# A hybrid layer on one core: opening loads in rows of 4 KB, and zeros multiplied on TensorE before the first block

## The chip, the core and the metric

The kernel runs on one NeuronCore of a Trainium2 chip. The core has a matrix engine (TensorE, PE in the profile, with its weight loads as PEld), a vector engine (VectorE, DVE), an engine for functions and copies (ScalarE, ACT), a general engine (GpSimd, POOL) and a synchronising engine (SyncE, SP) that here issues most loads. Each engine works through its own list of instructions in order and waits on semaphores for the others. Loads and stores go through 16 DMA engines. Work happens in SBUF, 128 partitions wide; TensorE writes into the eight banks of PSUM, each 128 partitions by 512 fp32 numbers.

The metric is the device time of one execution in microseconds. The kernel before took 1743.69 us in the median of three runs (1743.11, 1743.69, 1744.18).

## The reference: what is computed

One decoder layer, batch 1, 2048 positions, model width 1024, all in fp32, cut to what matters:

```python
cond = silu(c)                                  # one vector of 1024
mod = cond @ w_ada + b_ada                      # 6 x 1024: shift, scale, gate, twice
sh1, sc1, g1, sh2, sc2, g2 = split(mod, 6)

h = x * (1 + sc1) + sh1
z = h @ w_in                                    # 1024 -> 2048
gate_b, gate_c, v_conv, v_pool = split(z, 4)
y_conv = gate_b * short_conv(gate_c * v_conv, conv_w)      # causal, width 3
y_pool = multiscale_pool(v_pool, w_pool, pool_scale)       # windows 2, 4, 8, 16
mix = concat(y_conv, y_pool) @ w_out
x = layer_norm(alpha * x + (1 + g1) * mix)

h = x * (1 + sc2) + sh2
f = square(relu(h @ w_mlp_in)) @ w_mlp_out      # 1024 -> 4096 -> 1024
x = layer_norm(alpha * x + (1 + g2) * f)
```

Nothing of the layer can start before the first scales and shifts: they need `silu(c)`, and the dot product of it with rows of `w_ada`.

## The kernel before, in words

The sequence is worked on in two blocks of 1024 positions. The feature dimension lies on the partitions, 8 tiles of 128. The big products (input projection, output projection, MLP) are made on TensorE from operands that are split into a high and a low part (`split`, `mm3`: three matmuls for one product), and several of them in a scheme with sums of blocks that needs seven products of blocks instead of eight. Loads, splits and sums run beside the matmuls. The order of instructions on each engine is fixed when the kernel is built: the scheduler of the framework puts the instructions in an order by what it expects to be ready, and the program holds it in some places with `issue_after`.

The change touches only the opening of the program.

- `vecs` holds all small vectors, `c` among them. It is the first load. `in_turn` chains the loads that follow it on SP's queue in the order of the code.
- The first column tile of `w_ada` for the scale and for the shift of the first 128 features (`first`, two tiles of 128x1024) is loaded in four halves, then the first 128 rows of the first group's input weights (`w0`, 128x512), then the first 128 features of `x` (`x0`, in two halves of 128x512).
- `silu(c)` is made on ScalarE and VectorE. `spread` broadcasts it over all partitions with eight transposes on TensorE against the identity matrix, four into each of two PSUM banks (`cond_banks`).
- Behind the transposes, `WARM` = 7 multiplications of the identity by itself fill TensorE; nobody reads what they write.
- `ada_first` multiplies the tiles of `first` with the banks in four products on VectorE, each with a running sum (the sums go to `part`), and two small additions make the first scale and shift (`mod[:, 0:2]`).
- `first_group` then goes over the 8 feature tiles k. For each it needs the scale and shift of that tile; ScalarE makes the high part of `x * scale + shift` in two halves (`shifted`), VectorE the low part, and TensorE does 24 matmuls of 128x128 by 128x512 into 8 banks. While it does, `loads(k + 1)` brings the next tile's two rows of `w_ada`, weights and `x`, and VectorE makes the next scale and shift (`dot`, `biased`).

Names in the rows: `h_` are tiles of 128x1024 (the two of `first`, and operands), `r_` raw weights, `o_` other 128x1024 tiles (`x0` is one), `w_` split weights, `ps_` PSUM banks, `tmp` a scratch tile of 128x512.

Of the kernel before, what the change touches and what calls it, by code (L numbers as in the profile page):

```python
# [8 lines left out]
F32 = mybir.dt.float32  # L9
F32R = mybir.dt.float32r  # L10
AF = mybir.ActivationFunctionType
ALU = mybir.AluOpType

P = 128
# [3 lines left out]
H = 512  # L18
# [9 lines left out]
WINDOWS = (2, 4, 8, 16)  # L28
HALO = 16
HALF_SUMS = (1, 2, 3, 3, 3, 3, 3, 0)  # L30
WARM = 7
WW = T + HALO

SC1, SH1 = 0, 1
# [4 lines left out]


@with_exitstack
def tile_hybrid_layer(ctx: ExitStack, tc: tile.TileContext, xT, x, wada, vec, win0, win,
                      wins, wpool, wout, wmix, w1, w2, rows, out):
    nc = tc.nc

# [10 lines left out]
    def mk(p, shape, dt, tag, bufs):  # L56
        names[0] += 1
        return p.tile(shape, dt, name=f"{tag}_{names[0]}", tag=tag, bufs=bufs)

    def t_h(dt=F32R):  # L60
        return mk(big, [P, T], dt, "h", 28)

    def t_o(w=T, dt=F32):
        return mk(big, [P, w], dt, "o", 10)

    def t_w(dt=F32R):
        return mk(big, [P, T], dt, "w", 6)

    def t_r():
        return mk(big, [P, T], F32, "r", 5)  # L70

    def t_ps():
        return mk(pp, [P, H], F32, "ps", 8)
# [14 lines left out]
    def tt(out_, a, b_, op):  # L88
        return nc.vector.tensor_tensor(out_, a, b_, op=op)  # L89


    vecs = cp.tile([P, 104], F32, name="vecs")
# [3 lines left out]
    def in_turn(dst, src):  # L96
        if before:
            with tc.issue_after(before.pop()):
                d = nc.sync.dma_start(dst, src)  # L99
        else:  # L100
            d = nc.sync.dma_start(dst, src)
        before.append(d.ins)

    in_turn(vecs[:, :88], vec)
    halves = [slice(h * H, h * H + H) for h in range(2)]
    x0 = t_o()
    first = [t_h(F32), t_h(F32)]
    w0 = t_r()
    for hs in halves:
        for i, f in enumerate((SC1, SH1)):  # L110
            in_turn(first[i][:, hs], wada[f][:, hs])
    in_turn(w0[:, :H], win0[0])
    for hs in halves:
        in_turn(x0[:, hs], xT[0, 0][:, hs])
    silu = cp.tile([P, KD], F32, name="silu")
    nc.scalar.activation(silu, vecs[:, VX : VX + KD], AF.Sigmoid)
    tt(silu, silu, vecs[:, VX : VX + KD], ALU.mult)
# [3 lines left out]
    mod = cp.tile([P, 48], F32, name="mod")  # L121
    ident = cp.tile([P, P], F32, name="ident")
# [16 lines left out]
            nc.scalar.copy(dst[:, hs], banks[h])  # L139

    cond_banks = spread(silu)

    warm = t_ps()
    for _ in range(WARM):
        nc.tensor.matmul(warm[:, :P], ident, ident, start=True, stop=True)
    small = cp.tile([P, 6], F32, name="small")
    part, epst, c15 = small[:, 0:4], small[:, 4:5], small[:, 5:6]
    nc.gpsimd.memset(c15, 1.5)
# [21 lines left out]
    cond = t_o(D)  # L170

    def ada_first():
        for i in range(2):
            for h, hs in enumerate(halves):
                nc.vector.scalar_tensor_tensor(
                    first[i][:, hs], first[i][:, hs], 1.0, cond_banks[h], op0=ALU.mult, op1=ALU.mult,
                    accum_out=part[:, 2 * h + i : 2 * h + i + 1])
        nc.vector.tensor_tensor(part[:, 0:2], part[:, 0:2], vecs[:, 0:2], op=ALU.add)
        return nc.vector.tensor_tensor(mod[:, 0:2], part[:, 0:2], part[:, 2:4], op=ALU.add)

    opened = []
# [5 lines left out]
    def biased(f0, f1):  # L187
        return nc.vector.tensor_tensor(mod[:, f0:f1], acc[:, f0:f1], vecs[:, f0:f1], op=ALU.add)
# [14 lines left out]


    def shifted(dst, r, k, cs):
        return nc.scalar.activation(dst[:, cs], r[:, cs], AF.Identity, bias=mod[:, 2 * k + SH1 : 2 * k + SH1 + 1],  # L206
                                    scale=mod[:, 2 * k + SC1 : 2 * k + SC1 + 1])

    def load_m(src):
# [124 lines left out]
    def first_group(A):  # L334
        ps = {}

        def loads(k):
            rows_ = [t_h(F32) for _ in range(2)]
            wr, a = t_r(), t_o()
            for i, r in enumerate(rows_):  # L340
                in_turn(r, wada[2 * k + i])
            in_turn(wr[:, :H], win0[k])
            in_turn(a, xT[0, k])
            return rows_, wr, a

        done = ada_first()
        wr, a = w0, x0
        for k in range(KD):
            wt = t_w()
            hi, lo = t_h(), t_h()  # L350
            A.append((hi, lo))
            opened.append(done.ins)
            if k == 0:
                nc.scalar.copy(wt[:, :H], wr[:, :H])
            with tc.issue_after(done.ins):
                if k:
                    nc.scalar.copy(wt[:, :H], wr[:, :H])
                tt(wt[:, H:], wr[:, :H], wt[:, :H].bitcast(F32), ALU.subtract)
                for hs in halves:
                    high = shifted(hi, a, k, hs)  # L360
                    if k:
                        shifted(a, a, k, hs)
            if k + 1 < KD:
                rows_, wr_n, a_n = loads(k + 1)
            if k == 0:
                with tc.issue_after(high.ins):
                    for hs, bank in zip(halves, cond_banks):
                        nc.scalar.copy(cond[:, hs], bank)
            elif k + 1 < KD:
                done = dot(2 * k + 2, rows_[0])  # L370
            with tc.issue_after(done.ins):
                for hs in halves:
                    if k == 0:
                        sc, sh = (mod[:, 2 * k + i : 2 * k + i + 1] for i in (SC1, SH1))
                        nc.vector.tensor_scalar(a[:, hs], a[:, hs], sc, sh, op0=ALU.mult, op1=ALU.add)
                    low = tt(lo[:, hs], a[:, hs], hi[:, hs].bitcast(F32), ALU.subtract)
            if k + 1 < KD:
                with tc.issue_after(low.ins):
                    for i in range(k > 0, 2):
                        dot(2 * k + 2 + i, rows_[i])  # L380
                done = biased(2 * k + 2, 2 * k + 4)
                wr, a = wr_n, a_n
            for h, hs in enumerate(halves):
                for p in range(3):
                    for m in range(4):
                        if k == 0 and p == 0:
                            ps[m, h] = t_ps()
                        w = (H if p == 1 else 0) + m * P
                        nc.tensor.matmul(ps[m, h], wt[:, w : w + P], A[k][p // 2][:, hs],  # L389
                                         start=k == 0 and p == 0, stop=k == KD - 1 and p == 2)  # L390
        return ps
# [873 lines left out]
def _lay(inputs):  # L1265
    import numpy as np

    a = {k: np.asarray(v) for k, v in inputs.items()}
    x = a["x"].reshape(S, D)
    sh1, sc1, g1, sh2, sc2, g2 = [a["w_ada"][0].T.reshape(6, KD, P, D)[i] for i in range(6)]  # L1270
    vsh1, vsc1, vg1, vsh2, vsc2, vg2 = [a["b_ada"][0].reshape(6, KD, P)[i] for i in range(6)]

    def pairs(p, q):
        return np.stack([p, q], axis=1).reshape((2 * KD,) + p.shape[1:])

    wada = np.concatenate([pairs(sc1, sh1), g1, pairs(sc2, sh2), g2])
    bada = np.concatenate([pairs(vsc1, vsh1), vg1, pairs(vsc2, vsh2), vg2])
    conv = a["conv_w"][0].reshape(3, NG, P).transpose(1, 0, 2).reshape(3 * NG, P)
    vec = np.concatenate([bada, conv, a["pool_scale"][0].reshape(NG, P),
                          a["ln1_g"][0].reshape(KD, P), a["ln1_b"][0].reshape(KD, P),  # L1280
                          a["c"].reshape(KD, P)]).T
    w = a["w_in"][0].reshape(KD, P, 4, NG, P)[:, :, [3, 1, 2, 0]]
    return {
        "xT": x.T.reshape(KD, P, NB, T).transpose(2, 0, 1, 3),
        "x": x,
        "wada": wada,
        "vec": vec,
        "win0": w[:, :, :, 0].reshape(KD, P, 4 * P),
        "win": w.transpose(3, 2, 1, 0, 4).reshape(NG, 4, P, KD * P),
        "wins": w.reshape(2, 4, P, 2, 2, NG, P).transpose(5, 4, 0, 2, 3, 1, 6).reshape(NG, 4, P, T),  # L1290
        "wpool": a["w_pool"][0].transpose(0, 2, 1),
        "wout": a["w_out"][0][: D // 2].reshape(2, 2, P, 2, H).transpose(3, 0, 2, 1, 4),
        "wmix": a["w_out"][0][D // 2 :].reshape(NG, P, D),
        "w1": a["w_mlp_in"][0].reshape(2, 4, P, NC, 2, 2, P).transpose(3, 5, 0, 2, 4, 1, 6).reshape(NC, 4, P, T),
        "w2": a["w_mlp_out"][0].reshape(NC, 2, 2, P, 2, H).transpose(0, 2, 4, 3, 1, 5).reshape(NC, 4, P, T),
        "rows": np.stack([a["ln1_g"][0], a["ln1_b"][0], a["ln2_g"][0], a["ln2_b"][0]]),
    }
# [18 lines left out]
```

## Time and profile before

| what | value |
|---|---|
| median of three runs | 1743.69 us (1743.11 to 1744.18) |
| span of the profiled execution, first to last instruction | 1741.3 us |
| what lies around the span, median less span | 2.4 us |
| mean granted clock of TensorE | 0.997 |
| TensorE busy | 1726.9 us, 99% of the span |
| VectorE busy | 1265.7 us, 73% |
| ScalarE busy | 857.3 us, 49% |
| GpSimd busy | 191.7 us, 11% |
| the chain that ended last: TensorE's share | 98% |
| first real matmul | 10.07 us after the start |

The profiled execution has no time of its own beside its span; the 2.4 us are the distance of the span to the median of the runs. The profile's times count from the first instruction. A row of the timeline gives the start, the length of the group, engine, line of the code, operation, written tile `<-` read tiles, shape, how many; in square brackets stands the idle time of the engine ahead of it and what ended it. A row of a cut into stretches gives the stretch, its length, the busy time and count of each engine in the order PE, PEld, DVE, ACT, POOL, then the clock that TensorE was granted (1.00 is full), the busy share of the DMA engines and their rate in GB/s. In the view of one line of code the three figures are the shortest, median and longest duration in ns, then the first and last start.

### The profile page before, as it was taken

The page shows a single profiled execution, that of the slowest core. Times are in us where ns is not written, and L with a number is a line of the kernel's source. Part 1 is how long each engine was busy: PE and PEld are TensorE (multiplying, and loading weights), DVE is VectorE, ACT ScalarE, POOL GpSimd, SP SyncE. Part 2 cuts the span into 40 slices and gives each one's busy share as a digit, 9 for nine tenths or more (in the row PEclk, how much of TensorE's full clock was granted, in tenths as well). Part 3 has the DMA queues.
Part 4 walks back from the last instruction along what each step waited for, and adds up shares of the span by engine and source line. Part 5 has one row for each costly group of instructions (what it writes and reads, how often), then busy time and mean ns, then how long its engine had stood idle before and what let it go on. Part 6 is the DMA issues. An engine that isn't in the chain of part 4 may idle for free.

```text
span 1741.3 us, 21294 instructions
## 1 busy us (share of the span) xinstructions
PE 1726.9 (99%) x7678; PEld 1430.4 (82%) x7678; DVE 1265.7 (73%) x1617; ACT 857.3 (49%) x1158; POOL 191.7 (11%) x373
## 2 busy tenths in 40 slices
PE   8999999999999999999999999999999999999997
PEld 7888888888888888888888888888888888888886
DVE  7898698877777686759686789695565656465885
ACT  5323358554445554446573345765455564344451
POOL 0212221122222000000000000101000100000000
PEclk9999999999999999999999999999999999999999
DMA  9888777768888999887572266655434479677771
GB/s 377 332 334 326 302 260 275 271 253 322 315 332 312 378 419 340 295 281 269 200 265 82 100 230 218 226 193 199 143 133 145 158 269 371 194 248 251 269 256 49
DMA packets 136907, 443.70 MB, mean 255 GB/s; under 512 B 15713, under 2 KB 16225, under 8 KB 136801
## 3 DMA queue, kind: packets, MB, share of 16 engines
q1 hardware_dynamic: 94752, 292.90, 47.3%
q0 software_dynamic: 42048, 149.44, 22.4%
q8 instruction: 60, 0.98, 0.2%
q14 instruction: 47, 0.38, 0.1%
HBM read 307.54 MB, written 134.74 MB: 254 GB/s over the span
## 4 chain that ended last, share of the span: by engine, by line
PE 98%; DVE 1%; DMA 0%; ACT 0%; SPq 0%; issue 0%; DVEq 0%; ACTq 0%
PE ps L86 31%; PE ps L84 31%; PE ps L85 31%; PE ps L389 3%; PE ps L740 1%; DVE o L89 0%; DMA r<-in_win 0%; DVE o L1197 0%; DVE o L1191 0%; DVE st L709 0%; PE ps L132 0%; SPq L99 0%; ACT mv L700 0%; DVE mv L713 0%; ACT h L206 0%
## 5 line engine op out<-in xcount | busy, mean ns | idle before, releaser
L85 PE MATMUL ps<-h,w 128*128 128x512 f32 x1312 | 510.3, 389 | 0.0
L86 PE MATMUL ps<-h,w 128*128 128x512 f32 x1312 | 510.3, 389 | 0.0
L84 PE MATMUL ps<-h,w 128*128 128x512 f32 x1312 | 510.0, 389 | 0.0
L84 PE MATMUL ps<-h,h 128*128 128x512 f32 x1120 | 436.1, 389 | 0.0
L86 PE MATMUL ps<-h,h 128*128 128x512 f32 x1120 | 435.9, 389 | 0.0
L85 PE MATMUL ps<-h,h 128*128 128x512 f32 x1120 | 435.7, 389 | 0.0
L79 ACT CAST h<-r 128x1024 fp32r<-128x1024 f32 (+1 forms) x184 | 186.8, 1019 | 312.0 <-PE ps L85 201.2
L80 DVE TENSOR_TENSOR h<-r,h 128x1024 fp32r<-128x1024 f32 (+1 forms) x184 | 216.1, 1179 | 109.4 <-ACT h L79 109.2
L85 PEld LDWEIGHTS ps<-h,w 128*128 128x128 f32 x1312 | 246.3, 188 | 51.6 <-DVE h L80 0.4
L79 ACT CAST w<-r 128x1024 fp32r<-128x1024 f32 x156 | 164.3, 1053 | 252.4 <-PE ps L85 243.8
L86 PEld LDWEIGHTS ps<-h,w 128*128 128x128 f32 x1312 | 246.3, 188 | 51.2 <-DVE w L80 0.3
L84 PEld LDWEIGHTS ps<-h,w 128*128 128x128 f32 x1312 | 246.1, 188 | 51.4 <-issue 0.2
L80 DVE TENSOR_TENSOR w<-r,w 128x1024 fp32r<-128x1024 f32 x156 | 190.4, 1222 | 109.7 <-ACT w L79 108.3
L86 PEld LDWEIGHTS ps<-h,h 128*128 128x128 f32 x1120 | 210.2, 188 | 43.7
L85 PEld LDWEIGHTS ps<-h,h 128*128 128x128 f32 x1120 | 210.3, 188 | 43.7
L84 PEld LDWEIGHTS ps<-h,h 128*128 128x128 f32 x1120 | 210.3, 188 | 43.4 <-DVE o L859 0.3
L89 DVE TENSOR_TENSOR o<-o,o 128x512 f32<-128x512 f32 (+1 forms) x170 | 162.1, 958 | 57.2 <-DMA usum<-o 47.0
L89 DVE TENSOR_TENSOR o<-o,ps 128x512 f32<-128x512 f32 x156 | 105.5, 682 | 57.1 <-PE ps L86 56.3
L80 DVE TENSOR_TENSOR h<-w,h 128x1024 fp32r<-128x1024 f32 x112 | 136.4, 1218 | 6.2 <-ACT h L79 6.2
L79 ACT CAST h<-w 128x1024 fp32r<-128x1024 f32 x112 | 117.6, 1050 | 8.5 <-DMA w<-in_w 7.4
L965 POOL DMA_DIRECT2D usum<-o x112 | 59.9, 535 | 522.9 <-ACT o L962 226.4
L89 DVE TENSOR_TENSOR r<-r,r 128x1024 f32<-128x1024 f32 x60 | 73.4, 1223 | 22.0 <-DMA r<-in_w 15.5
(138 smaller groups left out, 1184.4 us busy)
## 6 DMA issues: line engine op xcount, KB each, us to landing
usum<-o POOLq DMA_DIRECT2D x112, 512.0 KB, 4.9
r<-usum SPq DMA_DIRECT2D x112, 512.0 KB, 5.0
w<-w2sum SPq DMA_DIRECT2D x64, 512.0 KB, 6.4
r<-in_w SPq DMA_DIRECT2D x60, 512.0 KB, 5.0
w<-in_w SPq DMA_DIRECT2D x48, 512.0 KB, 6.5
o<-in_w SPq DMA_DIRECT2D x72, 256.0 KB, 6.0
w2sum<-o POOLq DMA_DIRECT2D x64, 256.0 KB, 6.7
h<-in_wada SPq DMA_DIRECT2D x22, 512.0 KB, 9.6
```

Of the source, the lines that this page charges most:

```text
L79: high = nc.scalar.copy(hi, src)
L80: return high.ins, nc.vector.tensor_tensor(lo, src, hi.bitcast(F32), op=ALU.subtract).ins
L84: nc.tensor.matmul(ps, whi, xhi, start=first, stop=False, skip_group_check=goes_on)
L85: nc.tensor.matmul(ps, whi, xlo, start=False, stop=False, skip_group_check=goes_on)
L86: nc.tensor.matmul(ps, wlo, xhi, start=False, stop=last, skip_group_check=goes_on)
L89: return nc.vector.tensor_tensor(out_, a, b_, op=op)
L389: nc.tensor.matmul(ps[m, h], wt[:, w : w + P], A[k][p // 2][:, hs], start=k == 0 and p == 0, stop=k == KD - 1 and p == 2)
L740: nc.tensor.transpose(ps[:, t * P : t * P + P], R[4 * h + t][:, k * P : k * P + P], ident)
L965: nc.gpsimd.dma_start(usum[g, i], r)
```

## The change

Two things are done to the opening.

First, the loads. A new input `opening` of 3 x 128 x 1024 is laid out on the host: the first slab holds the left halves (columns 0 to 511) of the scale tile and of the shift tile side by side, the second the right halves, the third the first weights beside the left half of `x0`. Each is loaded by one DMA with rows of 4 KB, where there were seven DMAs with rows of 2 KB; the right half of `x0` still comes in a DMA of its own. Since a slab now holds one half of both tiles, the products of `ada_first` go by slab, and the first small addition stands inside the loop. In `first_group` the first x comes as two separate pieces (one inside `w0`), so the code there takes a list of pieces.

Second, TensorE. A tile of zeros is filled by VectorE at the program's start, and `warming(EARLY)` multiplies it by itself 10 times ahead of the code for `silu`; `warming(WARM)` does so 14 times behind the transposes in the code, where the 7 multiplications of the identity stood.

```diff
-WARM = 7
+EARLY, WARM = 10, 14
...
-    x0 = t_o()
     first = [t_h(F32), t_h(F32)]
-    w0 = t_r()
-    for hs in halves:
-        for i, f in enumerate((SC1, SH1)):
-            in_turn(first[i][:, hs], wada[f][:, hs])
-    in_turn(w0[:, :H], win0[0])
-    for hs in halves:
-        in_turn(x0[:, hs], xT[0, 0][:, hs])
+    w0, x0 = t_r(), t_o()
+    for r, src in zip((first[0], first[1], w0), opening):
+        in_turn(r, src)
+    in_turn(x0[:, H:], xT[0, 0][:, H:])
+    zeros = t_tmp()[:, :P]
+    nc.vector.memset(zeros, 0.0)
+    warm = t_ps()
+
+    def warming(n):
+        for _ in range(n):
+            nc.tensor.matmul(warm[:, :P], zeros, zeros, start=True, stop=True)
+
+    warming(EARLY)
     silu = cp.tile([P, KD], F32, name="silu")
...
     cond_banks = spread(silu)
-
-    warm = t_ps()
-    for _ in range(WARM):
-        nc.tensor.matmul(warm[:, :P], ident, ident, start=True, stop=True)
+    warming(WARM)
...
     def ada_first():
-        for i in range(2):
-            for h, hs in enumerate(halves):
+        for h in range(2):
+            for i, hs in enumerate(halves):
                 nc.vector.scalar_tensor_tensor(
-                    first[i][:, hs], first[i][:, hs], 1.0, cond_banks[h], op0=ALU.mult, op1=ALU.mult,
+                    first[h][:, hs], first[h][:, hs], 1.0, cond_banks[h], op0=ALU.mult, op1=ALU.mult,
                     accum_out=part[:, 2 * h + i : 2 * h + i + 1])
-        nc.vector.tensor_tensor(part[:, 0:2], part[:, 0:2], vecs[:, 0:2], op=ALU.add)
+            if h == 0:
+                nc.vector.tensor_tensor(part[:, 0:2], part[:, 0:2], vecs[:, 0:2], op=ALU.add)
         return nc.vector.tensor_tensor(mod[:, 0:2], part[:, 0:2], part[:, 2:4], op=ALU.add)
...
-        wr, a = w0, x0
+        wr, a = w0, [w0[:, H:], x0[:, H:]]
...
+    sides = np.concatenate([sc1[0], sh1[0]], axis=1).reshape(P, 2, 2, H)
+    opening = np.stack([np.concatenate([sides[:, 0, h], sides[:, 1, h]], axis=1) for h in range(2)]
+                       + [np.concatenate([w[0, :, :, 0].reshape(P, 4 * P), x.T[:P, :H]], axis=1)])
```

The order in which TensorE gets its instructions doesn't follow the code here, since the scheduler sets it. TensorE's first rows before, from the start of the program (L132 is a transpose, with the identity and `silu` as operands; L145 is the multiplication of the identity; L389 the layer's first matmuls; in brackets what an instruction waits for):

```order
L132 MATMUL ps_94<-ident,silu 128x128 [waits DVE_49,Pool_49]
L132 MATMUL ps_94<-ident,silu 128x128 x3
L132 MATMUL ps_99<-ident,silu 128x128 x4
L145 MATMUL ps_104<-ident 128x128 x7
L389 MATMUL ps_182<-h_159,w_158 128x512 [waits Activation_49]
```

The same place now (L117 is the multiplication of the zeros in `tmp_77`, L137 a transpose, L393 the layer's first matmuls):

```order
L117 MATMUL ps_79<-tmp_77 128x128 [waits DVE_49]
L117 MATMUL ps_79<-tmp_77 128x128 x23
L137 MATMUL ps_104<-ident,silu 128x128 [waits DVE_49,Pool_49]
L137 MATMUL ps_104<-ident,silu 128x128 x3
L137 MATMUL ps_109<-ident,silu 128x128 x4
L393 MATMUL ps_198<-h_175,w_174 128x512 [waits Activation_49]
```

All 24 multiplications of zeros, the 14 of the code's later place among them, stand ahead of the transposes, and nothing stands between the transposes and the layer's first matmul.

VectorE reads the banks of the transposes in its four products. Its rows before, from the spread vector's last multiplication to the first low part of the weights (L175 are the four products, L178 and L179 the two additions):

```order
L89 TENSOR_TENSOR silu<-silu,vecs 128x8 [waits Activation_49]
L175 SCALAR_TENSOR_TENSOR h_70,small<-h_70,ps_94 128x512 [waits DMAHW1_49,PE_49]
L175 SCALAR_TENSOR_TENSOR h_71,small<-h_71,ps_94 128x512 [waits DMAHW2_49]
L175 SCALAR_TENSOR_TENSOR h_70,small<-h_70,ps_99 128x512 [waits DMAHW3_49,PE_49]
L175 SCALAR_TENSOR_TENSOR h_71,small<-h_71,ps_99 128x512 [waits DMAHW4_49]
L178 TENSOR_TENSOR small<-small,vecs 128x2 [waits DVE_49]
L179 TENSOR_TENSOR mod<-small 128x2 [waits DVE_49]
L89 TENSOR_TENSOR w_158<-r_72,w_158 128x512 [waits DMAHW5_49,Activation_49]
```

The same stretch now (L177 the products, L181 and L182 the additions):

```order
L89 TENSOR_TENSOR silu<-silu,vecs 128x8 [waits Activation_49]
L177 SCALAR_TENSOR_TENSOR h_69,small<-h_69,ps_104 128x512 [waits DMAHW1_49,PE_49]
L177 SCALAR_TENSOR_TENSOR h_69,small<-h_69,ps_104 128x512
L177 SCALAR_TENSOR_TENSOR h_70,small<-h_70,ps_109 128x512 [waits DMAHW2_49,PE_49]
L181 TENSOR_TENSOR small<-small,vecs 128x2 [waits DVE_49]
L177 SCALAR_TENSOR_TENSOR h_70,small<-h_70,ps_109 128x512
L182 TENSOR_TENSOR mod<-small 128x2 [waits DVE_49]
L89 TENSOR_TENSOR w_174<-r_71,w_174 128x512 [waits DMAHW3_49,Activation_49]
```

The first small addition moved from behind the fourth product to between the third and the fourth, and two loads instead of four are waited for.

More of the change, by code (lines that the diff above doesn't have):

```diff
@@ L41, in tile_hybrid_layer @@
 @with_exitstack
-def tile_hybrid_layer(ctx: ExitStack, tc: tile.TileContext, xT, x, wada, vec, win0, win,
+def tile_hybrid_layer(ctx: ExitStack, tc: tile.TileContext, opening, xT, x, wada, vec, win0, win,
                       wins, wpool, wout, wmix, w1, w2, rows, out):
@@ L205, in shifted @@
     def shifted(dst, r, k, cs):
-        return nc.scalar.activation(dst[:, cs], r[:, cs], AF.Identity, bias=mod[:, 2 * k + SH1 : 2 * k + SH1 + 1],
+        return nc.scalar.activation(dst[:, cs], r, AF.Identity, bias=mod[:, 2 * k + SH1 : 2 * k + SH1 + 1],
                                     scale=mod[:, 2 * k + SC1 : 2 * k + SC1 + 1])
@@ L343, in loads @@
             in_turn(a, xT[0, k])
-            return rows_, wr, a
+            return rows_, wr, [a[:, hs] for hs in halves]
         done = ada_first()
-        wr, a = w0, x0
+        wr, a = w0, [w0[:, H:], x0[:, H:]]
         for k in range(KD):
@@ L358, in first_group @@
                 tt(wt[:, H:], wr[:, :H], wt[:, :H].bitcast(F32), ALU.subtract)
-                for hs in halves:
-                    high = shifted(hi, a, k, hs)
+                for x_, hs in zip(a, halves):
+                    high = shifted(hi, x_, k, hs)
                     if k:
-                        shifted(a, a, k, hs)
+                        nc.scalar.activation(x_, x_, AF.Identity, bias=mod[:, 2 * k + SH1 : 2 * k + SH1 + 1],
+                                             scale=mod[:, 2 * k + SC1 : 2 * k + SC1 + 1])
             if k + 1 < KD:
@@ L371, in first_group @@
             with tc.issue_after(done.ins):
-                for hs in halves:
+                for x_, hs in zip(a, halves):
                     if k == 0:
                         sc, sh = (mod[:, 2 * k + i : 2 * k + i + 1] for i in (SC1, SH1))
-                        nc.vector.tensor_scalar(a[:, hs], a[:, hs], sc, sh, op0=ALU.mult, op1=ALU.add)
-                    low = tt(lo[:, hs], a[:, hs], hi[:, hs].bitcast(F32), ALU.subtract)
+                        nc.vector.tensor_scalar(x_, x_, sc, sh, op0=ALU.mult, op1=ALU.add)
+                    low = tt(lo[:, hs], x_, hi[:, hs].bitcast(F32), ALU.subtract)
             if k + 1 < KD:
@@ L1282, in _lay @@
     w = a["w_in"][0].reshape(KD, P, 4, NG, P)[:, :, [3, 1, 2, 0]]
+    sides = np.concatenate([sc1[0], sh1[0]], axis=1).reshape(P, 2, 2, H)
+    opening = np.stack([np.concatenate([sides[:, 0, h], sides[:, 1, h]], axis=1) for h in range(2)]
+                       + [np.concatenate([w[0, :, :, 0].reshape(P, 4 * P), x.T[:P, :H]], axis=1)])
     return {
+        "opening": opening,
         "xT": x.T.reshape(KD, P, NB, T).transpose(2, 0, 1, 3),
```

## The prediction

> **What bounds the kernel now.** I first read the page: how busy TensorE is, and the chain that ended last.
>
> ```profile
> span 1741.3 us, 21294 instructions
> PE 1726.9 (99%) x7678; PEld 1430.4 (82%) x7678; DVE 1265.7 (73%) x1617; ACT 857.3 (49%) x1158; POOL 191.7 (11%) x373
> ```
>
> TensorE is busy for all but 14.4 us. The view of waits, asked for TensorE alone, says where it waits, and the timeline what stands around those places.
>
> ```profile
> PE ps L132 <- DVE silu L89: 3.2, 1, 3.2
> PE ps L389 <- ACT h L206: 2.1, 1, 2.1
> ...
> 3.15 1.94 PE L132 MATMUL ps<-ident,silu 128*128 128x128 f32 x8 [3.15 <-DVE silu L89]
> 4.89 3.05 PE L145 MATMUL ps<-ident 128*128 128x128 f32 x14
> 10.07 0.73 PE L389 MATMUL ps<-h,w 128*128 128x512 f32 x2 [2.13 <-ACT h L206]
> ```
>
> There are two waits in the whole run, both in the first 10.07 us: before the transposes that spread the condition vector over PSUM, and before the first matmul of the layer. From 10.07 us to the last matmul TensorE never waits again. So what moves the first real matmul moves the end by as much, as long as the operands of the next blocks are there; what only moves loads or VectorE work does nothing. The rest of the 14.4 us is the tail after the last matmul, which the change leaves alone.
>
> The second thing to read is the clock, in stretches that I cut where the granted clock changes:
>
> ```profile
> 0.84:4.25 3.41, 1.10 (x6) 1.13 (x7) 0.71 (x6) 1.39 (x2) 1.08 (x21) 1.00 0.60 169
> 4.25:7.66 3.41, 3.41 (x17) 3.41 (x17) 2.11 (x7) 0.00 (x0) 0.00 (x0) 1.00 0.90 270
> 7.66:11.08 3.42, 1.29 (x6) 0.95 (x6) 2.38 (x7) 2.49 (x4) 0.00 (x0) 1.00 1.04 401
> 11.08:14.49 3.41, 3.41 (x9) 2.67 (x8) 3.41 (x6) 1.22 (x3) 0.00 (x0) 0.50 1.04 422
> 14.49:17.90 3.41, 3.41 (x16) 2.81 (x15) 2.83 (x7) 2.87 (x5) 0.00 (x0) 1.00 1.03 416
> ...
> L389 PE MATMUL ps<-h,w 128*128 128x512 f32 x180 | 41.2, 390 | 0.0
> ...
> L145 PE MATMUL ps<-ident x14: 281/421/421, 4.9 to 7.7; 128*128 128x128 f32 x14
> ...
> 77.08 1.03 PE L132 MATMUL ps<-ident,mod 128*128 128x128 f32 x8
> 77.88 0.48 PE L84 MATMUL ps<-w,wp 128*128 128x512 f32 x1
> ```
>
> The first figure of a stretch is its length, the second TensorE's busy time; the third from the right is the granted clock. It was 0.50 for exactly one stretch of 3.41 us, after a stretch of the same length in which TensorE was busy for 1.29 of 3.42 us (38%), and it was full again after one that was busy throughout. Before 7.66 us the column's 1.00 is not to be trusted: passes of 128x128 are 0.214 us apart there (L145: 2.8 us from first to last start over 13 steps), while the eight at 77.08 us are 0.8 us over 7.3 steps or 0.109 us apart. So the program begins at half clock, and the last L145 pass, 281 ns instead of 421, marks the rise at 7.66. A matmul of 512 columns comes every 0.228 us at full clock (41.2 us for 180) and every 0.427 at half; one half-clock stretch filled with them costs 3.41 x (1 - 0.228/0.427) = 1.59 us.
>
> **The change, part by part.** *Order on TensorE.* The diff writes 10 zero multiplications ahead of the transposes and 14 behind. The instruction order quoted above shows all 24 ahead. One such multiplication is two passes (L145: 7 in the code, 14 in the trace), so 48 passes now stand in front of the transposes, and TensorE does matmuls in order. The condition vector, ready at 3.0 us, must wait for them; VectorE's first products read the PSUM banks that the transposes fill; ScalarE's first operand needs their sum. The cover that would cost these passes nothing, the wait for the loads, is on the wrong side of them.
>
> *Start of the zeros.* No row shows a fill on VectorE. GpSimd's fill of 128x128 took 0.20 us, and VectorE's pass over four times the columns 0.55; I take 0.2, nearest in size:
>
> ```profile
> 0.74 0.20 POOL masks.py:197 MEMSET ident<- 128x128 f32 x1 [0.29 <-POOLq L1305]
> ...
> 2.85 0.16 DVE L89 TENSOR_TENSOR silu<-silu,vecs 128x8 f32<-128x8 f32 x1
> ...
> 4.28 0.69 DVE L175 SCALAR_TENSOR_TENSOR h<-h,ps 128x512 f32<-128x512 f32 x1 [1.27 <-PE ps L132]
> 4.89 0.08 DVE L175 DVE_READ_ACCUMULATOR h<-h,ps 128x1 f32 x1
> 5.01 0.69 DVE L175 SCALAR_TENSOR_TENSOR h<-h,ps 128x512 f32<-128x512 f32 x1
> ...
> 6.94 0.69 DVE L175 SCALAR_TENSOR_TENSOR h<-h,ps 128x512 f32<-128x512 f32 x1 [1.24 <-DMA h<-in_wada]
> 7.56 0.08 DVE L175 DVE_READ_ACCUMULATOR h<-h,ps 128x1 f32 x1
> 7.56 0.68 DVE L175 SCALAR_TENSOR_TENSOR h<-h,ps 128x512 f32<-128x512 f32 x1
> ...
> 8.16 0.16 DVE L178 TENSOR_TENSOR small<-small,vecs 128x2 f32<-128x2 f32 x1
> 8.36 0.16 DVE L179 TENSOR_TENSOR mod<-small 128x2 f32<-128x2 f32 x1
> ...
> 8.51 0.62 ACT L354 CAST w<-r 128x512 fp32r<-128x512 f32 x1 [5.75 <-DMA r<-in_win]
> 9.21 1.52 ACT L206 ACTIVATE h<-o,mod 128x512 fp32r<-128x512 f32 x2
> 10.05 0.55 DVE L375 TENSOR_SCALAR o<-o,mod 128x512 f32<-128x512 f32 x1 [0.20 <-ACT h L206]
> ...
> 14.83 0.16 DVE L188 TENSOR_TENSOR mod<-acc,vecs 128x2 f32<-128x2 f32 x1
> ...
> 15.03 1.52 ACT L206 ACTIVATE h<-o,mod 128x512 fp32r<-128x512 f32 x2 [1.48 <-DVE mod L188]
> ```
>
> The engines start at 0.74; fill to 0.95; 0.14 from VectorE's end to TensorE's start (3.01 to 3.15): zeros from about 1.1 us. The ends for this term, 1.0 and 1.5, move the sum by 0.2 at most, since half of it is made good at full clock.
>
> *When they end* hangs on the rise of the clock. Case 1: it rises at 4.25, one stretch ahead of 7.66, because the zeros fill 3.15 of the 3.41 us before it (92%). Then (4.25 - 1.1)/0.214 = 14.7 passes are done, and 33.3 x 0.109 = 3.6 us are left: end at 7.9. Case 2: 92% is too little and it rises at 7.66: 30.7 passes, then 17.3 x 0.109 = 1.9: end at 9.55. All 48 at half clock would be 10.3 us.
>
> *From there to the first real matmul.* The fourth transpose is done 3 x 0.109 + 0.27 = 0.6 us later, and the products start 0.04 behind it: 0.64. Three steps of 0.61 to the fourth product (6.94 to 7.56) are 1.84, plus 0.12 for the small addition that the change now puts between the third and the fourth. From the fourth product 0.60 to the last addition (7.56 to 8.16), 0.20 to ScalarE (14.83 to 15.03), and 0.86 from its start to the first matmul (9.21 to 10.07). The old second addition (8.16 to 8.36, 0.19) is saved; it isn't in this sum. Together 4.26 us: first matmul at 12.15 in case 1 (+2.1), 13.8 in case 2 (+3.75).
>
> *The clock behind it.* TensorE is idle for 3.4 us between the last transpose and the first matmul (2.13 before). In case 1 the stretch 7.66 to 11.08 is filled for 1.1 us (31%, less than the 38% that dropped the clock before): half clock from 11.08. The stretch to 14.49 is filled for 2.3 us, 69%. If this is enough, matmuls lose 2.34 x 0.466 = 1.1 us, 0.5 less than now; if not, they run at half to 17.90 and lose 2.7, 1.1 more than now. Shift: +1.6 or +3.2. In case 2 the drop comes at 14.49 and costs the same 1.6 as now, or at 11.08 and costs 1.9: +3.75 or +4.1. [...]
>
> *The loads* are worth nothing in this sum, as the products now start at 8.5 us or later. The old first four loads had landed by 7.56 (L175's last product started then), the weight half at 8.51, the x halves by 9.21 and 9.97 (the two of ScalarE's 1.52 us); the new chain asks for them at 8.5, 9.7 (second row), 10.6 (weights, 0.62 ahead of ScalarE's 11.3) and 12.1. Were they no faster in 4 KB rows than now, each row complete only when its old last piece was, they would still be hidden by 1 us or more; if they land 2 us sooner, nobody is waiting. SP issues five opening loads instead of eight, so the second block's loads go out sooner; that too is cover, not gain.
>
> *The next block.* Its first operand came 5.82 us behind the first one's (9.21 to 15.03), so at 17.1 in case 1, ready for TensorE at 18.0. TensorE ends its 24 matmuls of the first block at 12.15 + 24 x 0.228 + 1.1 = 18.7 or later. No new wait; the shift stays whole to the end. VectorE's fill and the reciprocal behind it are done before 2.55, when the vectors come: nothing.
>
> **The sum.** Against the profiled execution's own span of 1741.3 us: +1.6 to +4.1, middle +2.8. The runs lie around this span plus 2.4 (median 1743.69), and the same shift is added to the median: 1746.5 us.
>
> **The rivals.** *Zeros don't count.* If the activity that lifts the clock is that of the data, 48 passes take 10.3 us (end at 11.4), transposes and first bank 3 x 0.214 + 0.42 + 0.04 = 1.1, and the matmuls start at 16.1 and at half clock: +6.0 and up to 1.6 more: 1749.7 to 1751.3. For it: in these rows no tile of zeros was ever multiplied. Against it: L145 lifted the clock with a matrix that is zero in all but its diagonal. [...]
>
> *Full clock throughout* (the other side). If the clock is full from the first zero and isn't dropped in the idle 3.4 us, the zeros end at 1.1 + 5.2 = 6.3, the first matmul starts at 10.6 (+0.5), and the half-clock stretch of 1.6 is gone: -1.1, 1742.6 us. With no drop it turns into a gain where the zeros end before 7.4, so where the clock rises before about 3.3 us. Against it: 0.214 us per pass up to 7.66, and a drop after a stretch that was 38% filled.
>
> *The order is as written*, so that the transposes stand between the tens and the fourteens: the products would start near 5.5 us, the first matmul near 9.4 with a clock still full, and 2.3 us would be gained: 1741.4. Against it stands the compiled order, which has no freedom left on the chip.
>
> **How the numbers follow.** Zeros ahead of the transposes, with a normal gate: 0.87; its own range is +1.2 to +4.4 (the shifts with 0.3 to either side for the start of the zeros and the spread of the runs, 1743.11 to 1744.18), and the value its middle, as 92% and 69% lie between the shown 38% and 100% and decide it. Zeros that don't count: 0.07. Full clock: 0.04. Order as written: 0.02. For 8 in 10 the range takes the first case with a little to both sides: 1744.6 to 1748.4. About 0.2%, 3.5 us, is what a measurement of this kernel can tell from no change. A quarter of the first case, the one with the late rise, lies above it, and all of the first rival: slower 0.29. The two gains stay below 3.5 us but for little: faster 0.02. Same 0.69.
>
> **What would show it.** In the changed profile: one group of 48 zero passes from about 1.1 to between 7.9 and 9.6 us, the transposes behind it, the products from 8.5 to 10.2 with TensorE as releaser and no DMA, the first matmul between 12.1 and 13.8 with an idle time of about 3.4 us before it, and one half-clock stretch over its first matmuls. Wrong would be a first matmul before 10.1 us, transposes that start at 3 us, a wait for a load ahead of the products, or new TensorE waits later on that swallow the shift.

## The result, and the profile after

| | median | runs |
|---|---|---|
| kernel before | 1743.75 us | 4, 1743.11 to 1744.18 |
| changed kernel | 1769.47 us | 4, 1769.10 to 1769.95 |
| ratio | 1.0151, 95% interval 1.0136 to 1.0165 | |

The change costs 25.7 us, nine times the forecast, and the opening explains only an eighth of it. The opening first, in TensorE's timeline of the changed kernel, with VectorE's and ScalarE's rows that lead to the first matmul:

```profile
1.06 7.12 PE L117 MATMUL ps<-tmp 128*128 128x128 f32 x48 [1.06 <-DVE tmp L112]
8.02 1.04 PE L137 MATMUL ps<-ident,silu 128*128 128x128 f32 x8
12.34 1.22 PE L393 MATMUL ps<-h,w 128*128 128x512 f32 x2 [3.29 <-ACT h L209]
...
8.65 0.69 DVE L177 SCALAR_TENSOR_TENSOR h<-h,ps 128x512 f32<-128x512 f32 x1 [5.55 <-PE ps L137]
10.56 0.68 DVE L177 SCALAR_TENSOR_TENSOR h<-h,ps 128x512 f32<-128x512 f32 x1
11.28 0.16 DVE L182 TENSOR_TENSOR mod<-small 128x2 f32<-128x2 f32 x1
...
7.54 0.62 ACT L357 CAST w<-r 128x512 fp32r<-128x512 f32 x1 [4.69 <-DMA r<-in_opening]
11.48 0.81 ACT L209 ACTIVATE h<-r,mod 128x512 fp32r<-128x512 f32 x1 [3.32 <-DVE mod L182]
```

All 48 zero passes stand ahead of the transposes. The first product waited 5.55 us for TensorE and not for a load; the cast of the first weights, which only needs a load, ran at 7.54 (8.51 before), and ScalarE then waited for VectorE until 11.48. The first matmul came at 12.34 us. The clock, cut at its edges again:

```profile
4.23:7.64 3.41, 3.41 (x32) 3.41 (x32) 0.00 (x0) 0.10 (x1) 0.00 (x0) 1.00 1.00 373
7.64:11.05 3.41, 1.41 (x13) 1.17 (x12) 2.40 (x8) 0.52 (x1) 0.00 (x0) 1.00 1.00 390
11.05:14.47 3.42, 2.13 (x5) 1.74 (x6) 2.95 (x8) 2.99 (x5) 0.00 (x0) 0.50 1.04 423
14.47:17.88 3.41, 3.41 (x9) 2.64 (x9) 3.38 (x8) 0.58 (x1) 0.00 (x0) 0.50 1.03 405
17.88:21.30 3.42, 3.42 (x16) 2.76 (x16) 2.86 (x5) 2.87 (x5) 0.00 (x0) 1.00 1.03 406
```

After a stretch filled for 41% (1.41 of 3.41 us) the clock fell to half; the next, filled for 62%, didn't lift it, and so it stayed down for two stretches instead of one. The second block of 24 matmuls started 3.3 us later than before (its first matmul at 20.55 against 17.24 us in the two traces).

The other 23 us are found nowhere as a wait. TensorE's waits in the changed kernel are two, and both lie in the opening; what changed is in the groups of matmuls. The page of the changed kernel, with the same stretch of 300 us of both kernels behind it (before, then after):

```profile
span 1767.5 us, 21358 instructions
PE 1754.4 (99%) x7712; PEld 1437.1 (81%) x7712; DVE 1268.4 (72%) x1618; ACT 857.1 (48%) x1158; POOL 191.1 (11%) x373
...
L86 PE MATMUL ps<-h,w 128*128 128x512 f32 x1312 | 517.4, 395 | 0.0
L85 PE MATMUL ps<-h,w 128*128 128x512 f32 x1312 | 517.3, 395 | 0.0
L84 PE MATMUL ps<-h,w 128*128 128x512 f32 x1312 | 517.2, 395 | 0.0
L84 PE MATMUL ps<-h,h 128*128 128x512 f32 x1120 | 436.0, 389 | 0.0
L86 PE MATMUL ps<-h,h 128*128 128x512 f32 x1120 | 435.9, 389 | 0.0
L85 PE MATMUL ps<-h,h 128*128 128x512 f32 x1120 | 435.7, 389 | 0.0
```

```profile
L85 PE MATMUL ps<-h,w 128*128 128x512 f32 x1312 | 510.3, 389 | 0.0
L84 PE MATMUL ps<-h,h 128*128 128x512 f32 x1120 | 436.1, 389 | 0.0
400.00:700.00 300.00, 300.00 (x1329) 248.24 (x1328) 216.61 (x243) 155.03 (x175) 53.08 (x99) 1.00 0.90 341
```

```profile
400.00:700.00 300.00, 300.00 (x1304) 245.01 (x1303) 219.29 (x247) 151.68 (x172) 56.72 (x106) 1.00 0.89 338
```

The three `h,w` groups, whose weights (the operand of 128x128) lie in `w` tiles and whose moving operand (128x512) lies in `h` tiles, went from 389 to 395 ns a matmul. The three `h,h` groups, with both operands in `h` tiles, did not change by a nanosecond. The clock is 1.00 and TensorE is busy for all 300 us, without a wait: it did 25 instructions fewer in the same time. Starts of neighbouring matmuls lie 226.8 ns apart before, and 232.5 in the `h,w` groups after (means over the whole trace, from the starts). This distance is called the pitch below. The difference is 5.7 ns for each of 3936 matmuls at L84 to L86, 22.2 us by their summed starts, and 1.0 us for the 168 of the first group behind the opening. With the 3.3 us this makes 26.5, and TensorE's last matmul starts at 1758.34 us instead of 1731.84.

### The profile page after: what moved, and what is told of

It reads as the page before. It is cut to its first block, busy times and chain, and to the rows that moved or that the text cites. A ratio compares the mean times of both kernels' runs of the same rounds, so it can differ in the third digit from the quotient of the medians.

```text
span 1767.5 us, 21358 instructions
## 1 busy us (share of the span) xinstructions
PE 1754.4 (99%) x7712; PEld 1437.1 (81%) x7712; DVE 1268.4 (72%) x1618; ACT 857.1 (48%) x1158; POOL 191.1 (11%) x373
## 3 DMA queue, kind: packets, MB, share of 16 engines
q0 software_dynamic: 42048, 149.44, 22.2%
## 4 chain that ended last, share of the span: by engine, by line
PE 98%; DVE 1%; ACT 0%; issue 0%; DVEq 0%
PE ps L84 31%; PE ps L85 31%; PE ps L86 31%; PE ps L393 3%; PE ps L744 1%; PE ps L117 0%; DVE o L89 0%; DVE o L1201 0%; DVE o L1195 0%; DVE st L713 0%; PE ps L137 0%; DVE h L177 0%; ACT mv L704 0%; DVE mv L717 0%; ACT h L209 0%
## 5 line engine op out<-in xcount | busy, mean ns | idle before, releaser
L86 PE MATMUL ps<-h,w 128*128 128x512 f32 x1312 | 517.4, 395 | 0.0
L85 PE MATMUL ps<-h,w 128*128 128x512 f32 x1312 | 517.3, 395 | 0.0
L84 PE MATMUL ps<-h,w 128*128 128x512 f32 x1312 | 517.2, 395 | 0.0
L84 PE MATMUL ps<-h,h 128*128 128x512 f32 x1120 | 436.0, 389 | 0.0
L86 PE MATMUL ps<-h,h 128*128 128x512 f32 x1120 | 435.9, 389 | 0.0
L86 PEld LDWEIGHTS ps<-h,w 128*128 128x128 f32 x1312 | 247.1, 188 | 58.1
L84 PEld LDWEIGHTS ps<-h,w 128*128 128x128 f32 x1312 | 247.1, 188 | 57.7
L84 PEld LDWEIGHTS ps<-h,h 128*128 128x128 f32 x1120 | 210.2, 188 | 43.8
L86 PEld LDWEIGHTS ps<-h,h 128*128 128x128 f32 x1120 | 210.2, 188 | 43.7
```

Source lines behind the costliest of these rows:

```text
L84: nc.tensor.matmul(ps, whi, xhi, start=first, stop=False, skip_group_check=goes_on)
L85: nc.tensor.matmul(ps, whi, xlo, start=False, stop=False, skip_group_check=goes_on)
L86: nc.tensor.matmul(ps, wlo, xhi, start=False, stop=last, skip_group_check=goes_on)
```

## The experiments

What do the `w` tiles have that the `h` tiles don't? The diff takes the first tiles in another order: `x0 = t_o()` stood ahead of `first` and `w0`, and now stands behind them. A pool lays out the slots of a kind when it is first asked for one. The addresses in the built programs, in bytes of each partition:

```
         first slot of each kind, in order
before   10 o at 18304   28 h at 59904    5 r at 174592   6 w at 195072
after    28 h at 18304    5 r at 132992  10 o at 153472   6 w at 195072
```

An `o` slot is 4160 bytes (some `o` tiles have 16 columns more), the others 4096. Ten of them make 41600 bytes, and this isn't a multiple of 512. While they lay ahead of `h` and `w`, they moved both alike; now they lie between the two. The distance from an `h` to a `w` slot was 0 modulo 512 and is now 128.

*Theory A*: the pitch of a matmul depends on where its weights start relative to its moving operand. *Theory B*, the rival: the zeros or the 4 KB loads cost the 23 us, through a state that they leave behind (clock, buffers, order), and the places don't matter.

**The old slots in the changed kernel.** One line is moved:

```diff
+    x0 = t_o()
     first = [t_h(F32), t_h(F32)]
-    w0, x0 = t_r(), t_o()
+    w0 = t_r()
```

> The changed kernel with one line moved: x0 is taken from its pool before the two first tiles again, so the 10 o slots lie ahead of the 28 h slots in SBUF as in the kernel before, and every h slot starts at the same place modulo 512 bytes as every w slot. Zeros, loads and the order of instructions stay as in the changed kernel. Theory A (the place of the h slots relative to the w slots sets the pitch of every matmul whose weights lie in w): the pitch goes from 232.5 back to 226.8 ns, and only the late first matmul is left, 3.3 us: 1747.0 us. Theory B (the cost comes with the zeros or the 4 KB loads, whatever the places): it stays at 1769 us.

Measured: 1745.86 us beside 1743.0 before, ratio 1.0014 (1.0005 to 1.0023). Its pitch is 226.7 ns. All but 2.9 us of the loss is gone, with all zeros and loads in place; and these 2.9 us are the opening, as a group of its page and the first matmul in its timeline show:

```profile
L85 PE MATMUL ps<-h,w 128*128 128x512 f32 x1312 | 510.3, 389 | 0.0
...
12.50 2.08 PE L394 MATMUL ps<-h,w 128*128 128x512 f32 x4 [3.29 <-ACT h L210]
```

**The new slots in the kernel before.** The other half of the test:

```diff
-    x0 = t_o()
     first = [t_h(F32), t_h(F32)]
     w0 = t_r()
+    x0 = t_o()
```

> The kernel before with only the order changed in which the first tiles are taken from their pool: the two h tiles and the r tile ahead of the o tile. No zeros, old loads, same instructions in the same order. Theory A: the pitch of the matmuls with weights in w goes from 226.8 to 232.5 ns, and about 4100 of them make 23 us: 1767 us. Theory B: 1743.7 us, unchanged.

Measured: 1768.06 us, ratio 1.0135 (1.0119 to 1.0151), though no instruction was added, removed or moved. The pitch in its profiled execution, the one of 1770.2 us, is 233.1 ns. Theory B falls, in both directions. From its page, a group with weights in `w` and one without:

```profile
L85 PE MATMUL ps<-h,w 128*128 128x512 f32 x1312 | 517.8, 395 | 0.0
L85 PE MATMUL ps<-h,h 128*128 128x512 f32 x1120 | 435.8, 389 | 0.0
```

**Relative or absolute.** In the changed kernel the `h` slots also lie lower than before. The first `w` tile is taken ahead of the first `o` tile, so that `w` follows `r`:

```diff
-    w0, x0 = t_r(), t_o()
+    w0 = t_r()
+    wt0 = t_w()
+    x0 = t_o()
...
-            wt = t_w()
+            wt = t_w() if k else wt0
```

> The changed kernel with its slot order, but the first w tile taken ahead of the o tile: the h slots stay where the changed kernel has them (384 bytes off a multiple of 512), the w slots move to the same place modulo 512, o comes last. Theory A (the place relative to each other): pitch 226.8 ns, 1745.9 us like the changed kernel with the old slots. Rival (the absolute place of the h slots, or their neighbours, costs the time): 1768 us.

Measured: 1746.3 us beside 1742.66, ratio 1.0019 (1.0009 to 1.0028), pitch 226.7 ns. `h` lies where it lies in the changed kernel, and the cost is gone: the place relative to `w` counts. What is left is the opening, as a group of its page and the first matmul in its timeline show:

```profile
L85 PE MATMUL ps<-h,w 128*128 128x512 f32 x1312 | 510.3, 389 | 0.0
...
13.73 1.90 PE L395 MATMUL ps<-h,w 128*128 128x512 f32 x4 [3.29 <-ACT h L211]
```

**How far apart.** In five single runs a small tile that the kernel has anyway is taken from the pool of the large ones, behind `h` and `r` and ahead of `w`; the `h` slots move down by its size and `w` stays. As an example the first:

```diff
-    pos = cp.tile([P, HALO], F32, name="pos")
+    pos = mk(big, [P, HALO], F32, "pos", 1)
```

> The kernel before with the small tile pos (64 bytes a partition) taken from the pool of the large tiles, behind the h and r slots and ahead of the w slots: the h slots move by 64 bytes, the w slots stay, so a w slot starts 64 bytes behind an h slot modulo 512. Theory A (what counts is whether the two start alike modulo 512): pitch above 226.8 ns for the matmuls with weights in w, by an unknown part of the 5.7 ns seen at 128; 3 to 12 ns, 1755 to 1792 us. Rival (only steps of 128 bytes, or the low address of the h slots, count): 1743 us.

> As the last, but with vhalo (256 bytes a partition) between: a w slot starts 256 bytes behind an h slot modulo 512. Theory A: slower again, with a pitch of its own; if the loss grows with the distance it is 11 ns, 1790 us, if any inequality costs the same it is 5.7 ns, 1766 us. Rival (the low address of the h slots counts): 1743 us, as the h slots lie where they did but for 256 bytes.

The next one puts the same tile of 256 bytes into the kernel with the new slots (the second experiment), so that 128 become 384.

> The kernel before with the slot order of the changed kernel (h, r, o) and vhalo between o and w: a w slot starts 384 bytes behind an h slot modulo 512, which is 128 bytes ahead. Theory A: if only the distance counts, as at 128: 232.5 ns, 1767 us; otherwise a pitch of its own above 226.8.

> The kernel before with acc (192 bytes a partition) taken behind the h and r slots and ahead of the w slots: a w slot starts 192 bytes behind an h slot. So far 64 bytes cost 6.6 ns a matmul, 128 and 384 cost 5.7, 0 and 256 nothing. If places count modulo 256, 192 is 64 bytes ahead and costs about 6 ns: 1768 us. If 256 was an exception of another kind, anything between.

> As the last, with uhalo (32 bytes a partition): a w slot starts 32 bytes behind an h slot, and o, h and r slots start at an odd multiple of 32. Places modulo 256: a pitch of 230 to 234 ns, 1756 to 1772 us. If only multiples of 64 are told apart: 1743 us.

| `w` starts behind `h` by (modulo 512) | time | pitch of `h,w` | pitch of `h,h` |
|---|---|---|---|
| 0 (kernel before) | 1743.75 us | 226.8 ns | 226.8 ns |
| 32 | 1770.9 us | 233.3 ns | 226.8 ns |
| 64 | 1769.7 us | 233.3 ns | 226.8 ns |
| 128 (changed kernel) | 1769.5 us | 232.5 ns | 226.8 ns |
| 128 (kernel before with the new slots) | 1768.1 us | 233.1 ns | 226.8 ns |
| 192 | 1751.8 us | 228.9 ns | 226.7 ns |
| 256 | 1743.7 us | 226.8 ns | 226.7 ns |
| 384 | 1764.7 us | 232.5 ns | 226.8 ns |

The pitches are means over the starts in the traces. They tell more than the times, which hold the opening of each execution too: in the runs on the kernel before, the second block of 24 matmuls started between 15.4 us (384) and 18.6 us (the new slots alone). 256 costs nothing, and 384 has the pitch of 128: 256 bytes more make no difference in either pair, so the distance seems to count modulo 256, as far as two pairs can show it. The two pitches at 128 are not two distances: as means over 96 matmuls on end, both traces have long parts near 232.4 ns and parts near 233.3; the changed kernel is mostly at the lower value and the other mostly at the higher. So less than 1 ns between two rows says nothing of the distance. My expectations for 256 (1766 or 1790 us) were wrong, as theory A had been put modulo 512. At 192 I expected the cost of 64; it was a third of that, so the cost isn't the same to both sides. The expectations for 64 (3 to 12 ns more), 32 (230 to 234 ns) and 384 (232.5) held. A group from the page of the run with 64, and one from that with 256:

```profile
L86 PE MATMUL ps<-h,w 128*128 128x512 f32 x1312 | 517.7, 395 | 0.0
```

```profile
L85 PE MATMUL ps<-h,w 128*128 128x512 f32 x1312 | 510.3, 389 | 0.0
```

**What the opening is worth on the old slots.** First with the order of the code: the 14 later zeros are held behind the last transpose.

```diff
-    warming(WARM)
+    with tc.issue_after(spread_last[0].ins):
+        warming(WARM)
```

> The changed kernel with the old slots, and the 14 later zero multiplications held behind the last transpose, so that TensorE has 10, the transposes, 14. By my working: the zeros end near 5.0 us, the products start near 5.6, the second slab (landed at 6.2 in the changed kernel) is no wait, ScalarE's first operand starts at 8.4 and the first matmul at 9.3; the 14 zeros fill TensorE to about 8.9, so the clock isn't dropped and the 1.6 us of the half-clock stretch are saved. Theory A: 1743.7 - 0.8 - 1.6 = 1741.3 us. Theory B: the zeros still cost some 20 us: above 1760 us.

Measured: 1740.88 us beside 1743.0, ratio 0.9987 (0.9978 to 0.9995). The first matmul came at 9.88 us, later than the 9.3 that I expected: the clock rose at 5.6 us in this execution, so the 10 zeros ended at 5.5 and still held up the transposes. The clock was then not dropped: it was 1.00 in the stretches from 5.61 to 9.03 and from 9.03 to 12.44 us, and 0.998 in the mean of the span.

Then the loads alone: no zeros, the 7 multiplications of the identity back in their place.

> The changed kernel with the old slots and without zeros: opening loads in rows of 4 KB, the identity multiplied 7 times behind the transposes as before. The slabs landed at 4.9, 6.2 and 7.5 us in the changed kernel, so the products run from 4.9 to 7.6 us, ScalarE's cast to 8.2, first matmul at 9.1 instead of 10.07: 1.0 us saved. The stretch from 7.64 to 11.05 is then filled for 67%; a stretch filled for 62% didn't bring the clock up and one filled for 92% did. If 67% doesn't hold the clock, the half-clock stretch stays: 1742.7 us; if it does: 1741.1 us. Theory B with the loads as cause: above 1760 us.

Measured: 1741.94 us beside 1743.0, ratio 0.9990 (0.9981 to 0.9999), with the first matmul at 8.78 us instead of 10.07. The loads that were worth nothing behind 24 zeros bring it forward by 1.3 us when nothing else stands in the way, and in this execution the clock held, over a stretch that was filled for 60%. The profiled execution is the fastest of the eleven, 2.2 us below their median; whether the clock held in the others isn't shown. The first matmul in its timeline, and its stretches cut at the clock's edges:

```profile
8.78 2.56 PE L388 MATMUL ps<-h,w 128*128 128x512 f32 x10 [1.36 <-ACT h L204]
...
6.58:9.99 3.41, 2.05 (x12) 1.68 (x12) 2.79 (x10) 2.60 (x5) 0.00 (x0) 1.00 0.98 371
9.99:13.41 3.42, 3.42 (x16) 2.83 (x16) 3.42 (x6) 1.02 (x2) 0.00 (x0) 1.00 1.04 419
```

Then both, with 4 zeros ahead instead of 10 (`EARLY, WARM = 4, 14`, the 14 held behind the transposes):

> The changed kernel with the old slots, 4 zero multiplications ahead of the transposes and the other 14 held behind them. Eight passes at half clock end at 2.8 us, before the transposes can start at 3.1, so the products wait for the first slab alone, as with the loads alone (first matmul at 8.8 us there), where 10 ahead made it 9.9. The 28 later passes end between 7.9 and 9.4, so that the clock holds. Theory A: 1 us less than with 10 ahead, 1739.9 us; if the passes end late, 1740.9, no gain.

Measured: 1740.62 us beside 1743.36, ratio 0.9985 (0.9976 to 0.9994). This is the lowest median of all versions, 0.15% below the kernel before and 1.6% below the changed kernel. The transposes start at 3.08 us, when `silu` is ready, and the products wait for the first slab alone; the 28 passes behind them end at 8.9 us and hold nothing up. But the slabs landed later than with the loads alone (the first product at 5.28 us instead of 4.85, the cast of the weights at 8.05 instead of 7.39), so that the first matmul is at 9.44 and the expected 1739.9 isn't reached. Against 10 zeros ahead the gain is within the noise. TensorE's timeline of this version:

```profile
3.08 1.94 PE L140 MATMUL ps<-ident,silu 128*128 128x128 f32 x8
4.81 4.10 PE L118 MATMUL ps<-tmp 128*128 128x128 f32 x28
9.44 1.88 PE L397 MATMUL ps<-h,w 128*128 128x512 f32 x7 [0.53 <-ACT h L213]
```

At last the zeros alone, 4 and 14, with the old loads and the old slots:

> The kernel before with its old loads and old slots, and zeros alone: 4 multiplications ahead of the transposes, 14 held behind them, in place of the 7 of the identity. If the loads set the first matmul, it stays near 10.07 us; the 28 later passes fill TensorE to between 7.9 and 9.5, so the half-clock stretch of 1.6 us goes: 1743.2 - 1.6 = 1741.6 us. If the clock is dropped nevertheless, or the zeros slow the loads: 1743 us or more.

Measured: 1741.42 us beside 1742.62, ratio 0.9996 (0.9987 to 1.0005). In its profile the first matmul is at 9.99 us and the clock isn't dropped, as expected (0.998 in the mean of the span, beside 0.997 before), but the gain can't be told from nothing.

## Why the prediction was wrong

*The step that failed* is the one called "The next block", with its sentence "No new wait; the shift stays whole to the end", and behind it the reading of the page: from "TensorE never waits again" I concluded that only what moves the first matmul moves the end. There was indeed no new wait. But the end is the first matmul plus some 7,500 pitches, and I took the pitch as given, since these instructions are the same in both programs. The edit `w0, x0 = t_r(), t_o()`, which stands in the diff, was priced at nothing without a word: it adds no instruction, and moves 28 + 5 + 10 slots. So the statement in the description that the change touches only the opening isn't right either: the slots stay moved to the end of the program. A term of 23 us was missing. The profile of before can't show it, as it has one distance only, but the built programs show that the addresses differ, and a change of addresses under a kernel in which 98% of the chain are matmuls should have stood among the rivals as a price that no row bounds.

*The opening* came out as forecast. The order with 48 passes ahead; the transposes behind them and the products with TensorE as releaser; first matmul at 12.34 us (forecast 12.15 in case 1); clock up at 4.23 us after a stretch filled for 93%, down after one of 41%, not lifted by 62%, so that the second branch of case 1 held: +3.2 us forecast, 3.3 measured in the trace, 2.9 by time in the run with the old slots. Taken by itself, with only the places put back, the change is 0.14% slower, 1745.9 us, which lies inside the range. Case 2 came too, in the run with `w` ahead, which begins with the same instructions: in its profiled execution the clock rose only at 7.14 us, the zeros ended at 9.57, the first matmul was at 13.73 (forecast 13.8), the half clock lasted one stretch, and the second block of matmuls started 3.7 us later than before (forecast 3.75). That 2.9 us by time come so close to the middle of +2.8 is in part luck, as that middle stands for no single case.

*The rivals.* The clock rose under zeros: in the changed kernel it did at 4.23 us, when TensorE had multiplied nothing else, from 1.06 us on. The clock at full throughout didn't happen: it was 0.50 from 11.05 to 17.88 us. The order as written did not happen either, but it was worth what I had put to it when it was forced: 2.1 us by the run with the transposes between the tens and the fourteens (2.3 forecast). Its parts differed: in that profile the first matmul came 0.2 us earlier and not 0.7, and the half-clock stretch of 1.6 us was gone.

*Where the clock rises* isn't set by the opening's instructions alone. The changed kernel, the one with the old slots and the one with `w` ahead all multiply zeros from 1.06 us on, and their clock rose at 4.23, 4.57 and 7.14 us. The kernel before and the six runs that have its opening show rises between 6.10 and 8.71 us, and one at 15.96. From the rise on it changed in steps of 3.41 us.

## What to carry to other kernels

When a change takes tiles from a pool in another order, or changes a tile's size, compare the addresses in the built programs before pricing the rest; on a kernel bound by matmuls like this one, let the slots of weights and of moving operands start at the same place modulo 256 bytes (226.8 ns a matmul at the distances 0 and 256 here, 228.9 to 233.3 at the five others), and put kinds of odd size ahead of both or behind both. A kernel in which TensorE never waits can still slow down: compare the mean duration of each group of matmuls, by operands (389 and 395 ns here), before looking for waits. And what fills TensorE before a dependency must be held by that dependency, or the scheduler may put it ahead of the work that was to hide it, as it did here.

## What the runs showed of the hardware

In these runs a 128x512 matmul with weights in `w` and its moving operand in `h` starts 226.8 ns after the one ahead if `w` starts 0 or 256 bytes behind `h` modulo 512, and 2 to 6.5 ns later (228.9 to 233.3 ns) at 32, 64, 128, 192 and 384 (the table above). The pitch depends on both places together: with `h` where the changed kernel has it and `w` moved, it went from 232.5 back to 226.7 ns. What in TensorE makes it so isn't shown. Nor do the runs show why 256 bytes more made no difference, why 192 is cheaper than 64, and why the pitch at 128 is 232.4 ns for hundreds of matmuls and 233.3 for hundreds of others. Over some 4100 matmuls these 0.9 ns are 3.7 us (an estimate from the two pitches); with the clock in the opening they may make the range of the kernel before with the new slots, 1764.8 to 1770.2 us in four runs, but only one of the four was traced.

In these traces the clock doesn't rise and fall by the same measure, and no single share of filling decides its rise. At half clock a stretch filled for 93% (changed kernel) and one of 80% (the run with 384) were followed by full clock; stretches of 62% (changed kernel), 68% (changed kernel with the old slots) and 82% (kernel before with the new slots) were not. At full clock a stretch of 60% (the loads alone) kept it, and those of 38% (kernel before) and 41% (changed kernel) lost it.
